# Four PSUM banks instead of two for the dense products behind the attention stage of a hybrid decoder layer

## The chip, the cores and the metric

The kernel runs on one core of one Trainium2 chip. The metric is device time in microseconds (us) of one execution; less is better. Engines are named as in the profile: PE (matrix products), DVE (VectorE), ACT (ScalarE), POOL (GpSimd), SP (SyncE, which here only issues DMAs).

## What is computed

One decoder layer over 1024 tokens of width 1024, in float32. A normalised input `h` goes through one wide projection; its columns feed an RWKV-7 time mixing, a causal depthwise convolution of width 31 with LayerNorm, and a cross-attention into 256 memory tokens. Each branch is projected back to 1024 columns, the three are merged by sigmoid gates, and an output projection with a residual and a final RMSNorm ends the layer. What matters here is the end:

```python
u = ((uf - um) * lax.rsqrt(uv + LN_EPS) * ln_g + ln_b)
u = jax.nn.silu(u) * jax.nn.silu(conv_gate)
y_conv = u @ w_proj_conv + b_proj_conv
...
y_mem = (att * jax.nn.silu(mem_gate)) @ w_proj_mem
gates = jax.nn.sigmoid(merge_logits).reshape(B, S, N_BRANCH, D_MODEL)
y = gates[:, :, 0] * y_rwkv + gates[:, :, 1] * y_conv + gates[:, :, 2] * y_mem
return x + y @ w_out, v_first
```

## The kernel before

Every dense product is one call of `g_dense` for one tile of 128 output columns. Operands are split into a high part and a low part (`hH`, `hL` for the input, `wh`, `wl` for the weight tile), and three matmuls per block of the inner dimension (high by high, low by high, high by low) keep float32 precision. A tile has two halves of 512 tokens (`e` = 0, 1). One half is a **group** here: 24 matmuls of 128x512 that add up in one PSUM bank `po`. The function `done` that is passed in then reads the bank (it evicts it, on ACT, DVE or both), and only after that may PE write the bank again.

PSUM has eight banks. `bank(tag, bufs)` (line 74) hands them out by tag: `d` 2, `g` 2, `ry` 2, `tr` 1, `sas` 1. All dense products use `d`, so a group's first matmul waits until the group two before it is evicted. Tag `g` serves the RWKV stage, the memory keys (line 870), the scores (line 938), the transposes of the probabilities (line 963) and the attention product (line 978); behind the attention nobody asks for it.

The weights come through `Stream`: a DMA brings `wf` (one buffer), ACT copies it to `wh` (line 123), DVE subtracts to `wl` (line 124). There are two buffers of `wh` and `wl`; the next tile's split is issued in the middle of a tile (`stream.ahead`).

From the last attention job on (`("att", 3)`) the program has five stages, and the numbers of groups below run over the first four:

- **cg**, groups 1 to 12: six tiles of the convolution gate. `done_cg` evicts with a tanh on ACT (line 927) and a DVE product (928), then writes to DRAM. Beside it run the last taps of the convolution (DVE, line 841) and `g_stats`: the channel mean (two products of PE into `ry`, line 995, that need `csum` from POOL, line 848) and the variance, column tile by column tile (`xs`: a load, DVE line 1006, ACT line 1008, POOL line 1013). The loads of `o_mem_d` are split into `oH`, `oL` (ACT line 270, DVE line 271).
- **pm**, groups 13 to 28: the memory projection. `done_pm` (line 1101) multiplies by the gate on DVE and writes `y1`. Beside it `g_ln` normalises 16 half tiles `xv`: loads, DVE lines 1047, 1051, 1056, 1058, ACT lines 1054, 1055, 123, POOL line 124.
- **pc**, groups 29 to 44: the convolution projection, on the output of `g_ln`. `done_pc` evicts on ACT (line 1138), then DVE. Beside it the loads of `o_rwkv_d` (one buffer `ost`) are split by ACT line 270 and DVE line 271, and half of the output weights (`woH`, `woL`).
- **pr**, groups 45 to 60: the RWKV projection, evicted by DVE (line 1157).
- **wo**: the output product, 16 groups of 24 matmuls through `mm3` (line 212), evicted by DVE (line 1189).

Within one engine the instructions run in the order in which they stand. That order is made when the program is built: the generators are interleaved by written costs, and the framework then orders the instructions engine by engine.

Of the kernel before, what the change touches and what calls it, by code (L numbers as in the profile page):

```python
# [62 lines left out]
def hybrid_kernel(ctx: ExitStack, tc: tile.TileContext, x: bass.AP, mem: bass.AP, wt: bass.AP,  # L63
# [10 lines left out]
    def bank(tag, bufs=1):  # L74
        return ps.tile([P, HS], F32, name=tag, tag=tag, bufs=bufs)
# [37 lines left out]
    def rsqrt(out_ap, in_ap, mul, add):  # L113
        pool.tensor_scalar(out=out_ap, in0=in_ap, scalar1=mul, scalar2=add, op0=ALU.mult, op1=ALU.add)
        p0 = in_ap.shape[0]
        n = in_ap.shape[1]
        base = 0 if p0 == P else P - p0
        pool.tensor_tensor(out=out_ap, in0=out_ap, in1=nhalf[base:P, 0:n], op=ALU.pow)
# [88 lines left out]
    def mm3(po, terms):  # L207
        n = 3 * len(terms)
        i = 0
        for (lh, ll, rh, rl) in terms:  # L210
            for l, r in ((lh, rh), (lh, rl), (ll, rh)):
                pe.matmul(po, lhsT=l, rhs=r, start=(i == 0), stop=(i == n - 1))  # L212
                i += 1
# [52 lines left out]
    def g_load_o(op, src, scale, oH, oL, dt):  # L266
        for k in range(KT):
            st = op.tile([P, S], F32, name="ost", tag="ost", bufs=1)
            nc.sync.dma_start(out=st, in_=src[k])
            act.activation(oH[:, k, :], st, AF.Copy, scale=scale)  # L270
            dve.scalar_tensor_tensor(out=oL[:, k, :], in0=st, scalar=scale, in1=oH[:, k, :].bitcast(F32),  # L271
                                     op0=ALU.mult, op1=ALU.subtract)
            yield dt

    def split_tiles(op):
        return op.tile([P, KT, S], F32R, name="oH"), op.tile([P, KT, S], F32R, name="oL")


    def g_dense(idx, done, rh=None, rl=None, pre=None):
        wh, wl = stream.get(idx)  # L280
        rh, rl = (hH, hL) if rh is None else (rh, rl)
        for e in range(2):
            if pre is not None:
                pre(e)
            po = bank("d", 2)
            sl = slice(e * HS, (e + 1) * HS)
            n = 0
            for k in range(KT):
                ks_ = slice(k * P, (k + 1) * P)
                for l, r in ((wh, rh), (wh, rl), (wl, rh)):  # L290
                    pe.matmul(po, lhsT=l[:, ks_], rhs=r[:, k, sl], start=(n == 0), stop=(n == 3 * KT - 1))  # L291
                    n += 1
                    if n % 4 == 0 and n < 3 * KT:
                        yield
            if e == 0:
                stream.ahead()
            done(e, po)
            yield
# [21 lines left out]

    late = {}
    lo_gen = g_dense(T_LO, lambda e, po: late["lo"](e, po))
    with tc.tile_pool(name="prep", bufs=1, reuse_waits="tile") as pl:
        for i, _ in enumerate(g_norm(x, S, "g_norm", pl, hH, hL)):
# [4 lines left out]
    with tc.tile_pool(name="rk", bufs=1, reuse_waits="tile") as rk:  # L329
# [103 lines left out]
        def tile_job(kind, j):  # L433
            if kind == "lo":
                late["lo"] = done_lo
                return lo_gen
            if kind == "k":
                return g_dense(T_K + j, done_shift(KS, j, T_K, "ks", 2))
            if kind == "r":
                return g_dense(T_R + j, done_shift(RS, j, T_R, "rs", 3))  # L440
            if kind == "v":
                return g_dense(T_V + j, done_shift(VS, j, T_V, "v", 2))
            if kind == "g":
                return g_dense(T_RG + j, done_sg(j))
            return g_dense(T_M0 + j, done_m(j))
# [347 lines left out]
    def later(name, gen):  # L793
        lanes.setdefault(name, [0.0, []])[1].append(gen)

    def run(gen):
        for dt in gen:
            background(dt or 0.85)
# [9 lines left out]
    def opened(stack, name, **kw):  # L808
        return stack.enter_context(tc.tile_pool(name=name, bufs=1, reuse_waits="tile", **kw))
# [255 lines left out]
    for n_, i_ in att_jobs:  # L1065
        run(g_dense(kinds[n_] + i_, done[n_](i_)) if n_ in done else other[n_](i_))
        if (n_, i_) == ("att", 3):
            at_stack.close()
            kv_stack.close()
            pm = AT["pm"] = opened(pm_stack, "pm")  # L1070
            mean = pm.tile([P, S], F32, name="mean")
            rstd = pm.tile([P, S], F32, name="rstd")
            AT["ones"] = pm.tile([P, P], F32, name="ones")
            dve.memset(AT["ones"], 1.0)
            omH, omL = split_tiles(pm)
            later("conv", g_stats(mean, rstd))
            later("load", g_load_o(pm, o_mem_d, 0.5, omH, omL, 6.0))
# [38 lines left out]
    def g_wo(pl, fh, hi, lo, dt):  # L1116
        fs = slice(fh * HS, (fh + 1) * HS)
        for k in range(KT):
            st = w0.tile([P, HS], F32, name="wst", tag="wst", bufs=2)
            nc.sync.dma_start(out=st, in_=wt[T_WO + k][:, fs])  # L1120
            split_sb(st, hi[:, k, :], lo[:, k, :])
            yield dt

    def wo_tiles(pl):
        return pl.tile([P, KT, HS], F32R, name="woH"), pl.tile([P, KT, HS], F32R, name="woL")
# [42 lines left out]
    with tc.tile_pool(name="wo1", bufs=1, reuse_waits="tile") as w1:  # L1168
        wo.append(wo_tiles(w1))
        gf = w1.tile([P, D], F32, name="gf")  # L1170
        nc.scalar.dma_start(out=gf, in_=gfin.broadcast_to([P, D]))
        xr = []
        for t in range(KT):
            xt = w1.tile([P, D], F32, name=f"xr{t}")
            nc.scalar.dma_start(out=xt, in_=x[t * P:(t + 1) * P, :])
            xr.append(xt)
        ss = w1.tile([P, KT, 2], F32, name="fss")
        e0 = w1.tile([P, KT], F32, name="fe")
        rs = w1.tile([P, KT], F32, name="frs")
        g1 = g_wo(w1, 1, *wo[1], 0.0)  # L1180
        for fh in range(2):
            fs = slice(fh * HS, (fh + 1) * HS)
            oh, ol = wo[fh]
            for t in range(KT):
                tl = slice(t * P, (t + 1) * P)
                po = bank("d", 2)
                mm3(po, [(yH[:, k, tl], yL[:, k, tl], oh[:, k, :], ol[:, k, :]) for k in range(KT)])
                next(g1, None)
                dve.tensor_tensor(out=xr[t][:, fs], in0=xr[t][:, fs], in1=po, op=ALU.add)
                sq = w1.tile([P, HS], F32, name="sq", tag="sq", bufs=2)  # L1190
                act.activation(sq, xr[t][:, fs], AF.Square, accum_out=ss[:, t, fh:fh + 1])
                if fh == 0:
                    pool.tensor_scalar(out=e0[:, t:t + 1], in0=ss[:, t, 0:1], scalar1=1.0 / D, scalar2=RMS_EPS,
                                       op0=ALU.mult, op1=ALU.add)
                if fh == 1:
                    rsqrt(rs[:, t:t + 1], ss[:, t, 1:2], 1.0 / D, e0[:, t:t + 1])
                    for h_ in range(2):
                        hs_ = slice(h_ * HS, (h_ + 1) * HS)
                        dve.scalar_tensor_tensor(out=xr[t][:, hs_], in0=xr[t][:, hs_], scalar=rs[:, t:t + 1],
                                                 in1=gf[:, hs_], op0=ALU.mult, op1=ALU.mult)  # L1200
                        (nc.sync, nc.scalar)[h_].dma_start(out=out[tl, hs_], in_=xr[t][:, hs_])
# [45 lines left out]
```

## Time and profile before

| | before |
|---|---|
| median of 3 runs | 1961.04 us (1960.19 to 1962.81) |
| the profiled execution, its own time | 1960.84 us |
| its span in the trace | 1959.0 us |
| PE busy | 1848.2 us, 94% |
| DVE busy | 1411.1 us, 72% |
| ACT busy | 693.2 us, 35% |
| POOL busy | 226.5 us, 12% |
| mean clock granted to PE | 0.991 |

PE is the busiest engine by far, and its matmuls are pipelined: the busy time counts each from its own start to its modelled end. What a stage loses on PE is therefore read from the idle time before a matmul and from the start of one group to the start of the next. The span lies 1.84 us under the execution's own time.

### The profile page before, as it was taken

To read this page: it belongs to the slowest core of one execution; us is meant where nothing else is said; L and a number is where in the kernel's file an instruction comes from. 1 tells how busy PE (TensorE), PEld (TensorE's weight loads), DVE (VectorE), ACT (ScalarE), POOL (GpSimd) and SP (SyncE) were. 2 spreads that over 40 slices of the span, in tenths; PEclk is the share of its full clock that TensorE was granted. 3 is DMA by queue.
4 is the path that set the end of the run, shared out by engine and by line. 5 is a ranking of instruction groups with operands and counts; after the bars stand their busy time and mean duration, and the time that the engine had idled before them with its cause. 6 is when DMAs were issued, how large, how long until landed. Compare 5 with 4: busy or idle time off the path is not lost. (4 is left out here: it accounts for less than half of the span.)

```text
span 1959.0 us, 30018 instructions
## 1 busy us (share of the span) xinstructions
PE 1848.2 (94%) x11412; PEld 1472.8 (75%) x11412; DVE 1411.1 (72%) x3028; ACT 693.2 (35%) x1303; POOL 226.5 (12%) x311
## 2 busy tenths in 40 slices
PE   6999998989899899989999999999999999999998
PEld 5777766767676676667788888888888787778887
DVE  6667787777778777787636998898999748644423
ACT  6334343443344344334334313232313435432121
POOL 2201111111111111111000000000000213100001
PEclk9999999999999999999999999999999999999999
DMA  4232212122121212212224411212123646775332
GB/s 147 58 97 63 71 36 68 54 61 68 48 86 36 66 56 58 71 42 79 71 78 140 132 46 42 75 54 76 54 76 108 233 163 221 256 252 164 129 129 86
DMA packets 127936, 188.61 MB, mean 96 GB/s; under 512 B 64432, under 2 KB 66608, under 8 KB 127792
## 3 DMA queue, kind: packets, MB, share of 16 engines
q1 hardware_dynamic: 122704, 178.11, 29.0%
q10 hardware_dynamic: 4768, 8.07, 1.1%
q8 instruction: 89, 1.46, 0.3%
q0 software_dynamic: 320, 0.52, 0.1%
q14 instruction: 55, 0.45, 0.1%
HBM read 139.92 MB, written 46.20 MB: 95 GB/s over the span
## 5 line engine op out<-in xcount | busy, mean ns | idle before, releaser
L291 PE MATMUL d<-hH,wh 128*128 128x512 f32 x1552 | 626.0, 403 | 6.8 <-DVE cg L928 4.4
L291 PE MATMUL d<-hH,wl 128*128 128x512 f32 x1552 | 621.8, 401 | 0.0
L291 PE MATMUL d<-hL,wh 128*128 128x512 f32 x1552 | 619.1, 399 | 0.0
L291 PEld LDWEIGHTS d<-hH,wh 128*128 128x128 f32 x1552 | 294.1, 189 | 63.6 <-DVE cg L928 5.7
L291 PEld LDWEIGHTS d<-hH,wl 128*128 128x128 f32 x1552 | 294.1, 190 | 59.4 <-issue 0.2
L291 PEld LDWEIGHTS d<-hL,wh 128*128 128x128 f32 x1552 | 294.1, 189 | 56.2 <-issue 0.2
L841 DVE SCALAR_TENSOR_TENSOR ac<-up,wdw,ac 128x1024 f32<-128x1024 f32 x240 | 308.2, 1284 | 11.8 <-ACT ac L838 6.0
L123 ACT CAST wh<-wf 128x1024 fp32r<-128x1024 f32 x137 | 143.6, 1049 | 324.1 <-PE d L291 304.3
L124 DVE TENSOR_TENSOR wl<-wf,wh 128x1024 fp32r<-128x1024 f32 x137 | 176.8, 1291 | 95.7 <-ACT wh L123 95.4
L291 PE MATMUL d<-oH,wh 128*128 128x512 f32 x384 | 152.5, 397 | 11.4 <-DVE mg L1101 7.4
L291 PE MATMUL d<-oH,wl 128*128 128x512 f32 x384 | 151.4, 394 | 0.0
L291 PE MATMUL d<-oL,wh 128*128 128x512 f32 x384 | 151.4, 394 | 0.0
L583 DVE TENSOR_TENSOR W<-W,tm 128x60 f32<-128x60 f32 (+24 forms) x496 | 112.4, 227 | 10.0
L580 DVE TENSOR_TENSOR tm<-W,U 128x60 f32<-128x60 f32 (+24 forms) x496 | 107.7, 217 | 11.1
L706 ACT ACTIVATE sp<-s,pc 128x128 f32<-128x128 f32 x120 | 48.3, 402 | 174.8 <-DVE s L713 137.6
L291 PEld LDWEIGHTS d<-oH,wh 128*128 128x128 f32 x384 | 72.9, 190 | 30.4 <-ACT y L1138 5.1
L710 PEld LDWEIGHTS sas<-sav,tk 128*128 128x128 f32 x240 | 38.4, 188 | 67.5 <-DVE sav L703 49.2
L710 PE MATMUL sas<-sav,tk 128*128 128x128 f32 x240 | 54.1, 307 | 34.1 <-DVE sav L703 32.4
L291 PEld LDWEIGHTS d<-oH,wl 128*128 128x128 f32 x384 | 72.8, 190 | 16.1
L291 PEld LDWEIGHTS d<-oL,wh 128*128 128x128 f32 x384 | 72.8, 189 | 15.4
L713 DVE SCALAR_TENSOR_TENSOR s<-sas,pc,sp 64x64 f32<-64x64 f32 x240 | 67.6, 282 | 21.5 <-PE sas L710 16.1
L703 DVE TENSOR_TENSOR sav<-ry,Y 64x128 f32<-64x128 f32 x128 | 36.8, 288 | 43.4 <-ACT Y L668 26.5
(277 smaller groups left out, 2608.7 us busy)
## 6 DMA issues: line engine op xcount, KB each, us to landing
wf<-in_wt_dram SPq DMA_DIRECT2D x137, 512.0 KB
g_d<-gt SPq DMA_DIRECT2D x48, 256.0 KB
U<-ud SPq DMA_DIRECT2D x64, 128.0 KB
nxt<-in_x_dram SPq DMA_DIRECT2D x8, 512.0 KB
o_rwkv_d<-o SPq DMA_DIRECT2D x16, 256.0 KB
cv_d<-ac SPq DMA_DIRECT2D x8, 512.0 KB
o_mem_d<-om SPq DMA_DIRECT2D x16, 256.0 KB
xs<-cv_d SPq DMA_DIRECT2D x8, 512.0 KB
```

Of the source, the lines that this page charges most:

```text
L123: act.copy(hi, src)
L124: (eng or dve).tensor_tensor(out=lo, in0=src, in1=hi.bitcast(F32), op=ALU.subtract)
L291: pe.matmul(po, lhsT=l[:, ks_], rhs=r[:, k, sl], start=(n == 0), stop=(n == 3 * KT - 1))
L580: dve.tensor_tensor(out=tv, in0=W[:, 0:m, i:i + 1].broadcast_to([NG * 32, m, n]), in1=U[:, i:i + 1, i + 1:32].broadcast_to([NG * 32, m, n] ...
L583: dve.tensor_tensor(out=wv_, in0=wv_, in1=tv, op=ALU.add)
L703: dve.tensor_tensor(out=sav[own, cc, :], in0=ry[own, cs], in1=Y[own, c // 2, :], op=ALU.add)
L706: act.activation(sp, S0, AF.Copy, scale=pc[:, c:c + 1])
L710: pe.matmul(sn[:, 0:P], lhsT=tk[:, cc, :], rhs=sav[:, cc, :], start=True, stop=True)
L713: dve.scalar_tensor_tensor(out=S1[vsl, vsl], in0=sn[vsl, vsl], scalar=pc[vsl, c:c + 1], in1=sp[vsl, vsl], op0=ALU.mult, op1=ALU.add)
L841: dve.scalar_tensor_tensor(out=ac, in0=up[:, tap:tap + S], scalar=wdw[:, tap * 8 + j:tap * 8 + j + 1], in1=ac, op0=ALU.mult, op1=ALU.add)
```

## The change

A counter `banks` gives each dense group a tag in turn. Up to the last attention job the list of tags is `("d",)`, so nothing changes there. From then on it is `("d", "g")`: the groups alternate between the two banks of `d` and the two of `g`, and a group's first matmul waits for the eviction of the group four before it. `g_dense` and the output product both use it.

```diff
+    banks = {"n": 0, "tags": ("d",)}
+
+    def dense_bank():
+        banks["n"] += 1
+        return bank(banks["tags"][banks["n"] % len(banks["tags"])], 2)
+
     def g_dense(idx, done, rh=None, rl=None, pre=None):
...
-            po = bank("d", 2)
+            po = dense_bank()
...
         if (n_, i_) == ("att", 3):
             at_stack.close()
             kv_stack.close()
+            banks["tags"] = ("d", "g")
...
-                po = bank("d", 2)
+                po = dense_bank()
                 mm3(po, [(yH[:, k, tl], yL[:, k, tl], oh[:, k, :], ol[:, k, :]) for k in range(KT)])
```

The framework's order of instructions differs from before in one stretch only, the cg stage: on PE, DVE, ACT and SP. POOL's order is the same everywhere, and from the pm stage on so is that of the other engines, but for the name of the bank. Two places follow. In the changed kernel line numbers between 285 and 1069 are 7 higher, and 8 higher behind that.

PE, in group 5: the two products for the channel mean (`ry<-csum,ones`) between the group's matmuls. Before:

```order
L291 MATMUL d<-hH,wh 128x512
L291 MATMUL d<-hL,wh 128x512
L995 MATMUL ry<-csum,ones 128x512 x2
L291 MATMUL d<-hH,wl 128x512
L291 MATMUL d<-hH,wh 128x512
L291 MATMUL d<-hL,wh 128x512
```

Now:

```order
L298 MATMUL g<-hL,wh 128x512
L298 MATMUL g<-hH,wl 128x512
L298 MATMUL g<-hH,wh 128x512
L298 MATMUL g<-hL,wh 128x512
L1002 MATMUL ry<-csum,ones 128x512 x2
L298 MATMUL g<-hH,wl 128x512
```

The pair stood behind the eighth matmul of its group and now stands behind the eleventh.

DVE, in the cg stage, from the low part of the weights of its fifth tile (groups 9 and 10) to that of its sixth (`wl`; `xs` is the variance, `cg` an eviction, `oL` a split of `o_mem_d`). Before:

```order
L124 TENSOR_TENSOR wl<-wf,wh 128x1024
L1006 TENSOR_TENSOR xs<-xs,mean 128x1024
L928 SCALAR_TENSOR_TENSOR cg<-cg,d 128x512
L1006 TENSOR_TENSOR xs<-xs,mean 128x1024
L271 SCALAR_TENSOR_TENSOR oL<-ost,oH 128x1024
L124 TENSOR_TENSOR wl<-wf,wh 128x1024
L928 SCALAR_TENSOR_TENSOR cg<-cg,d 128x512
```

Now:

```order
L124 TENSOR_TENSOR wl<-wf,wh 128x1024
L1013 TENSOR_TENSOR xs<-xs,mean 128x1024
L271 SCALAR_TENSOR_TENSOR oL<-ost,oH 128x1024
L935 SCALAR_TENSOR_TENSOR cg<-cg,g 128x512
L1013 TENSOR_TENSOR xs<-xs,mean 128x1024
L271 SCALAR_TENSOR_TENSOR oL<-ost,oH 128x1024
L935 SCALAR_TENSOR_TENSOR cg<-cg,d 128x512
L1013 TENSOR_TENSOR xs<-xs,mean 128x1024
L124 TENSOR_TENSOR wl<-wf,wh 128x1024
L1013 TENSOR_TENSOR xs<-xs,mean 128x1024
```

Counted from the first `wl`, one `xs`, one `cg` and one `oL` more stand ahead of the second than before. The first `wl` itself has one `oL` less ahead of it, so the sixth tile's weights have moved behind one more `xs`, the sixth, and one more eviction.

## Rows read from the trace of the kernel before

**Rows 1.** Waits of PE, 1505 to 1960 us: us in total, times, longest.
```profile
PE d L291 <- DVE mg L1101: 7.4, 5, 2.8
PE d L291 <- DVE cg L928: 4.4, 3, 2.7
PE d L291 <- ACT y L1138: 4.0, 2, 2.6
```
**Rows 2.** Timeline of PE, cg stage: start, us; in brackets idle before and releaser.
```profile
1523.78 0.50 PE L291 MATMUL d<-hH,wh 128*128 128x512 f32 x1 [0.91 <-DVE cg L928]
1531.65 1.98 PE L995 MATMUL ry<-csum,ones 128*128 128x512 f32 x4 [0.30 <-POOL csum L848]
1561.74 0.50 PE L291 MATMUL d<-hH,wh 128*128 128x512 f32 x1 [2.69 <-DVE cg L928]
1575.34 0.50 PE L291 MATMUL d<-hH,wh 128*128 128x512 f32 x1 [0.78 <-DVE cg L928]
1580.91 0.40 PE L291 MATMUL d<-oH,wh 128*128 128x512 f32 x1
```
**Rows 3.** Timeline of PE, pm stage: first matmuls of groups 22 to 27.
```profile
1634.97 0.40 PE L291 MATMUL d<-oH,wh 128*128 128x512 f32 x1
1641.22 0.47 PE L291 MATMUL d<-oH,wh 128*128 128x512 f32 x1 [0.49 <-DVE mg L1101]
1648.35 0.50 PE L291 MATMUL d<-oH,wh 128*128 128x512 f32 x1 [1.30 <-DVE mg L1101]
1655.44 0.47 PE L291 MATMUL d<-oH,wh 128*128 128x512 f32 x1 [1.22 <-DVE mg L1101]
1662.82 0.50 PE L291 MATMUL d<-oH,wh 128*128 128x512 f32 x1 [1.56 <-DVE mg L1101]
1671.51 0.48 PE L291 MATMUL d<-oH,wh 128*128 128x512 f32 x1 [2.83 <-DVE mg L1101]
```
**Rows 4.** The same, pc stage: first matmuls of groups 30, 36, 38, 39 and 40.
```profile
1689.77 0.39 PE L291 MATMUL d<-oH,wh 128*128 128x512 f32 x1
1723.96 0.50 PE L291 MATMUL d<-oH,wh 128*128 128x512 f32 x1 [1.39 <-ACT y L1138]
1737.90 0.80 PE L291 MATMUL d<-oH,wh 128*128 128x512 f32 x1 [2.60 <-ACT y L1138]
1744.81 0.39 PE L291 MATMUL d<-oH,wh 128*128 128x512 f32 x1
1750.25 0.39 PE L291 MATMUL d<-oH,wh 128*128 128x512 f32 x1
```
**Rows 5.** Windows: busy us of each engine in each stretch, PEclk, DMA share, GB/s.
```profile
1560.00:1570.00 10.00, 8.26 (x29) 6.64 (x30) 6.95 (x6) 4.64 (x6) 3.49 (x2) 0.83 0.82 254
1670.00:1680.00 10.00, 8.49 (x30) 6.79 (x31) 9.44 (x12) 5.24 (x7) 3.25 (x3) 0.83 0.64 222
1736.00:1746.00 10.00, 8.10 (x30) 6.59 (x31) 5.13 (x8) 4.45 (x6) 0.00 (x0) 0.83 0.80 250
1780.00:1790.00 10.00, 10.00 (x45) 8.13 (x44) 2.75 (x5) 0.97 (x2) 0.00 (x0) 1.00 0.57 184
```
**Rows 6.** Timeline of POOL and DVE, cg stage.
```profile
1529.19 2.40 POOL L848 TENSOR_TENSOR csum<-csum,ac 128x1024 f32<-128x1024 f32 x1 [60.52 <-DVE ac L841]
1561.60 1.21 DVE L1006 TENSOR_TENSOR xs<-xs,mean 128x1024 f32<-128x1024 f32 x1
1573.47 1.21 DVE L124 TENSOR_TENSOR wl<-wf,wh 128x1024 fp32r<-128x1024 f32 x1
```
**Rows 7.** Timeline of DVE and ACT, pm and pc: weights, and what stands beside them.
```profile
1663.38 1.23 DVE L124 TENSOR_TENSOR wl<-wf,wh 128x1024 fp32r<-128x1024 f32 x1 [0.62 <-ACT wh L123]
1669.12 1.65 DVE L1047 TENSOR_TENSOR xv<-xv,mean 128x512 f32<-128x512 f32 x1 [1.00 <-DMA xv<-cv_d]
1677.97 1.73 DVE L124 TENSOR_TENSOR wl<-wf,wh 128x1024 fp32r<-128x1024 f32 x1
1725.11 1.22 DVE L124 TENSOR_TENSOR wl<-wf,wh 128x1024 fp32r<-128x1024 f32 x1
1734.78 1.23 DVE L124 TENSOR_TENSOR wl<-wf,wh 128x1024 fp32r<-128x1024 f32 x1 [3.25 <-ACT wh L123]
1736.22 1.06 ACT L270 ACTIVATE oH<-ost 128x1024 fp32r<-128x1024 f32 x1 [1.47 <-DMA ost<-o_rwkv_d]
```

## The prediction

> **What bounds the kernel now.** I read the waits of PE first, from the end of the attention on. All of PE's idle time at the dense products there is laid to three evictions: 7.4 us behind `mg`, 4.4 behind `cg`, 4.0 behind `y`, ten waits and 15.8 us together [rows 1]. The timeline then shows where: three in cg [rows 2], five in pm [rows 3], two in pc [rows 4]. Each stands before the first matmul of a group, so it is the bank of the group two before that was not yet read. In pr and wo there is none: PE runs without idle time at 1780 to 1790 [rows 5].
>
> The windows show a second loss. Around the three longest waits (2.69, 2.83, 2.60 us) the granted clock is 0.83 over 10 us, against 1.00 in a stretch without waits [rows 5]: the clock fell from 2.4 to 1.2 GHz for a while, and each time 0.17 x 10 = 1.7 us of work at full rate is lost, 5.1 together. The wait of 1.56 us [rows 3] has no such fall behind it (the windows name just three).
>
> A third, small loss is the restart. Group 24 starts 7.13 us after group 23, of which 1.30 is the wait ahead of it [rows 3]; from group 22 to 23 it is 6.25 with a wait of 0.49. An undisturbed group takes 5.6 in this stage, so about 0.22 are lost beside the wait; ten waits make 2.2. In pc an undisturbed group takes 1750.25 - 1744.81 = 5.44 [rows 4], which is 0.227 for each of 24 matmuls.
>
> So the whole loss that hangs on the banks is 15.8 + 5.1 + 2.2 = 23.1 us. What the change gives is this less what PE meets next.
>
> **The change, part by part.** It adds and removes no instruction that computes or moves data; no durations change. It lets PE be four groups ahead of the evictions instead of two. The banks of `g` are free: the attention product is their last user. In pr and wo I cost it at nothing, since PE does not wait there. A group's eviction takes 0.6 to 0.7 us on one engine; the lateness comes from the queues in front of it, and they stay. So I walk along PE from group to group and ask at each tile whether the bank or the weights (`wl`, which the third matmul of a tile reads, 0.47 after its first) come last.
>
> *cg.* The three waits go: 0.91 + 2.69 + 0.78 = 4.4, with one fall of the clock 1.7 and three restarts 0.7, 6.8 in all. Part of the first comes back at once. The products for the channel mean wait for `csum`, which POOL ends at 1529.19 + 2.40 = 1531.6 [rows 6] whatever PE does. PE gets there 0.91 + 0.22 earlier, but three matmuls (0.68) now stand ahead that stood behind, so its wait grows from 0.30 to 0.75: 0.45 back. Next are the weights of group 11. Their `wl` stands behind the sixth `xs` now, which ran at 1561.60 for 1.21 [rows 6]; with 1.2 for itself `wl` ends by 1564.0. Group 11 would start at 1563.7 (group 13 at 1580.91 - 6.35 [rows 2], less two groups of 5.44) and needs it at 1564.2: no wait, but no room either. The weights of group 13 ended at 1573.47 + 1.21 = 1574.7 [rows 6], and are needed at 1580.91 - 6.35 + 0.47 = 1575.0 [rows 2]: again just in time. Of 6.35 I take **6.0**; the bounds are 3 (each of these two late by some 1.6, an `xs` with its load) and 6.35.
>
> *pm and pc, in the times of before.* What DVE and ACT do here is started by PE once: the variance goes through two small products between groups 14 and 17, where PE does not wait, so the whole chain of `g_ln` comes earlier by the 6.0 of cg and no more. From there DVE sets its own pace: at 1670 to 1680 it is busy 9.44 of 10 us [rows 5], and its gaps are waits for loads of `xv` [rows 7]. ACT in pc is held by the loads of `o_rwkv_d`, one behind the other through one buffer, and the evictions and weights stand behind them in its queue [rows 7]. So I leave every time of DVE and ACT as it is and move PE alone:
>
> - Group 23 starts at 1634.97 + 5.6 = 1640.6, groups 24 to 26 follow without a wait (the evictions that they need now are two groups older; the worst of before was 2.83 late, two groups are 11.2). Group 27 starts at 1663.0.
> - It opens a tile, and its `wl` ends at 1663.38 + 1.23 = 1664.6 [rows 7]. Needed at 1663.4: 1.2 lost and 0.2 for the restart. Group 29 starts at 1663.0 + 11.2 + 1.4 = 1675.6.
> - Its `wl` ends at 1677.97 + 1.73 = 1679.7 [rows 7], needed at 1676.0: 3.7 + 0.2 lost. Group 30 starts at 1675.6 + 5.4 + 3.9 = 1684.9; before it was 1689.77 [rows 4]. Here 4.9 are gained.
> - Groups 31 to 36 take 5.44 each; the waits ahead of groups 36 and 38 (1.39 and 2.60) were for banks that are no longer needed then. Group 37 starts at 1723.0. Its `wl` ends at 1725.11 + 1.22 = 1726.3 [rows 7], needed at 1723.5: 2.9 + 0.2 lost.
> - Group 39 starts at 1736.9; its `wl` is there at 1734.78 + 1.23 = 1736.0 [rows 7]. Group 40 starts at 1742.4, and the eviction that it needs is the one that let group 38 go at 1737.9 before. Before, group 40 started at 1750.25 [rows 4]: **7.8** gained, with no wait behind it.
>
> So of ten waits for banks three come back as waits for weights, at groups 27, 29 and 37. The last two are long enough for the clock to fall (2.60 was, 1.56 was not). After group 29 that would be made up by the wait at group 37; after group 37 it would cost 1.7, which leaves 6.1. I take 7.8, since the wait at 37 comes in two pieces, for `wh` and for `wl`.
>
> Sum: 6.0 + 7.8 = **13.8 us** off the profiled execution's 1960.84, whose span is 1959.0; it lies 0.2 under the median of the runs, 1961.04. Forecast for the median: **1947.2 us**. The bounds of the terms, 3 + 6.1 and 6.35 + 7.8, give 1947 to 1952.
>
> **The rivals.**
>
> *A, every wait goes and nothing takes its place.* All but 0.45 of 23.1: 1938.4 us. For it: no wait for weights is among PE's rows now [rows 1]. Against it: those weights were on time only because PE was late, and at group 29 the row misses by 3.7. The Trainium skill ("Perfetto Trace Analysis", Optimizing Tensor Performance, Matmuls) says that independent groups should rotate through banks so that the evacuation of one overlaps the next; by that alone this would be the outcome. The rows with `wl` speak against it. Chance 0.10.
>
> *B, the wait is renamed.* DVE and ACT are the pace, and PE, let off the banks, waits for weights at nearly every tile from group 25 on; only the first cg waits are gained, some 3 us: 1958. For it: the weights of groups 27, 29 and 37 are already late in my walk. Against it: those of group 39 and of all later tiles are not, and in pc the bank that PE needs is two groups older. The Trainium skill ("TensorE: Matmul & The Clock Gate", HAM oscillation — how this bites in real kernels) tells of a kernel in which PSUM double-buffering gave no further gain; by that case it would be 1961. Rows 1 disagree, for here PE does wait for banks. Chance 0.07.
>
> *C, slower: the new order on DVE in cg.* The weights of group 11 now stand behind the sixth `xs`, those of group 13 behind the eighth as before. An `xs` hangs on a load, ACT and POOL: sixth to eighth took 10.7 us (1561.60 to the `wl` directly behind the eighth at 1573.47, less 1.2) [rows 6], 5.4 each. If this chain slips, PE stands, and its clock falls too. Three steps late make 3 x 5.4 + 3 x 1.7 = 21.3, against 13.8 won: 1968.5. It decides from two steps on (14.2). Against it: the chain's loads depend on POOL, whose order is unchanged. Chance 0.03.
>
> **How the numbers follow.** My forecast has 0.80. About 0.2% (3.9 us) is what a measurement of this kernel can tell from no change. B lies within that, C above; so faster 0.90, same 0.07, slower 0.03. For the range I take 1941.5 to 1953: below, half way to A; above, the bound of 1952 and a little.
>
> **What would show it.** Right: PE's waits for `cg`, `mg` and `y` are gone or under 2 us together; new waits of PE stand at groups 27, 29 and 37 with ACT `wh` or DVE `wl` as releaser, some 8 us in all; the wait at the channel mean is near 0.75; stage pm starts 6 us earlier and group 40 nearly 14; pr and wo take as long as before. Wrong: waits for `mg` or `y` still there (then the evictions lag by more than four groups); waits for weights in cg (rival C); no waits at groups 27 and 29 (rival A, with DVE earlier than I leave it); or the granted clock below 1.00 in more than three places.

## The result, and the profile after

| | before | the change | ratio (95%) |
|---|---|---|---|
| median, first comparison | 1962.29 us (1960.19 to 1962.91, 6 runs) | 1949.73 us (1945.27 to 1951.05, 6 runs) | 0.9933 (0.9920 to 0.9946) |
| median, repeated | 1961.70 us (1957.44 to 1966.86, 17 runs) | 1951.38 us (1948.09 to 1953.43, 6 runs) | 0.9946 (0.9930 to 0.9961) |
| the profiled execution of the first | 1960.84 us, span 1959.0 | 1949.77 us, span 1947.8 | |
| mean clock granted to PE | 0.991 | 0.993 | |

The changed kernel is faster by 12.6 us in the first comparison and by 10.3 in the second. The forecast was 1947.2 us, with a range of 1941.5 to 1953.

The span is 11.2 us shorter. Where these went is read from the first matmuls of groups 1, 13, 30 and 40, the places at which the prediction counts the gain. The stretches between them are called cg, pm and pc here; the second holds all of pm and the first group of pc:

| us | cg (1 to 13) | pm (13 to 30) | pc (30 to 40) | group 40 to the end |
|---|---|---|---|---|
| before | 74.56 | 108.86 | 60.48 | 208.75 |
| the change | 68.79 | 105.00 | 58.58 | 208.55 |
| gained | 5.8 | 3.9 | 1.9 | 0.2 |

Together that is 11.7; group 1 itself starts 0.5 later than before, ahead of anything that the change touches. Two falls of the clock fewer than before (one in place of three, some 1.7 us each) are a part of the gain.

The waits of PE in the changed kernel from 1490 to 1960 us (us in total, times, longest), which answer to [rows 1]:

```profile
PE g L298 <- ACT wh L123: 5.3, 3, 2.2
PE g L298 <- DVE wl L124: 2.1, 3, 1.2
PE ry L1002 <- POOL csum L855: 1.0, 1, 1.0
```

Not one wait for `cg`, `mg` or `y` is left; 7.4 us of waits for weights stand there instead. The timeline of PE shows where. These lines are the beginnings of groups 1 and 13, the channel mean, then the first and third matmuls of groups 27, 29 and 37 and the first of groups 30 and 40; they answer to [rows 2 to 4]:

```profile
1506.88 0.40 PE L298 MATMUL g<-hH,wh 128*128 128x512 f32 x1
1532.32 1.98 PE L1002 MATMUL ry<-csum,ones 128*128 128x512 f32 x4 [0.99 <-POOL csum L855]
1575.67 0.40 PE L298 MATMUL g<-oH,wh 128*128 128x512 f32 x1
...
1659.13 0.50 PE L298 MATMUL g<-oH,wh 128*128 128x512 f32 x1 [1.24 <-ACT wh L123]
1660.39 0.50 PE L298 MATMUL g<-oH,wl 128*128 128x512 f32 x1 [0.53 <-DVE wl L124]
1673.55 0.50 PE L298 MATMUL g<-oH,wh 128*128 128x512 f32 x1 [2.16 <-ACT wh L123]
1675.51 0.51 PE L298 MATMUL g<-oH,wl 128*128 128x512 f32 x1 [1.23 <-DVE wl L124]
1680.67 0.39 PE L298 MATMUL d<-oH,wh 128*128 128x512 f32 x1
1720.83 0.68 PE L298 MATMUL g<-oH,wh 128*128 128x512 f32 x1 [1.92 <-ACT wh L123]
1722.31 0.79 PE L298 MATMUL g<-oH,wl 128*128 128x512 f32 x1 [0.38 <-DVE wl L124]
1739.25 0.39 PE L298 MATMUL d<-oH,wh 128*128 128x512 f32 x1
```

Each of the three tiles waits twice: for the rounded weights `wh`, which ACT makes, and 1.3 to 2.0 us later for the remainder `wl`, which DVE makes from `wh`. The timelines of POOL, DVE and ACT say why these are late (they answer to [rows 7]). At group 29 it begins with an operation of `g_ln` on DVE, which takes 1.67 us at 1670.23, while POOL works. ACT's cast of `oH` waits 1.95 us for it, and the cast of `wh` stands behind that one and ends at 1672.45 + 1.04 = 1673.49. Then `wl` ends at 1673.74 + 1.71 = 1675.45, again beside an operation of POOL. At group 37 the cast of `wh` stands on ACT behind the cast of `ost`, which waits 1.22 us for its load.

```profile
1670.06 1.29 POOL L124 TENSOR_TENSOR oL<-xv,oH 128x512 fp32r<-128x512 f32 x1 [4.10 <-ACT oH L123]
1672.62 1.74 POOL L124 TENSOR_TENSOR oL<-xv,oH 128x512 fp32r<-128x512 f32 x1 [1.28 <-ACT oH L123]
...
1670.23 1.67 DVE L1065 TENSOR_TENSOR xv<-xv,lsg 128x512 f32<-128x512 f32 x1
...
1673.74 1.71 DVE L124 TENSOR_TENSOR wl<-wf,wh 128x1024 fp32r<-128x1024 f32 x1
...
1671.93 0.62 ACT L123 CAST oH<-xv 128x512 fp32r<-128x512 f32 x1 [1.95 <-DVE xv L1065]
1672.45 1.04 ACT L123 CAST wh<-wf 128x1024 fp32r<-128x1024 f32 x1
...
1718.21 1.06 ACT L270 ACTIVATE oH<-ost 128x1024 fp32r<-128x1024 f32 x1 [1.22 <-DMA ost<-o_rwkv_d]
...
1719.74 1.03 ACT L123 CAST wh<-wf 128x1024 fp32r<-128x1024 f32 x1
```

The windows around the three tiles, columns as in [rows 5]:

```profile
1657.00:1667.00 10.00, 8.23 (x34) 6.05 (x33) 7.97 (x10) 5.03 (x7) 3.10 (x2) 1.00 0.63 224
1672.00:1682.00 10.00, 7.23 (x30) 5.67 (x31) 5.31 (x7) 4.86 (x7) 3.03 (x2) 1.00 0.77 238
1718.00:1728.00 10.00, 7.70 (x28) 5.47 (x27) 6.69 (x8) 4.82 (x6) 0.00 (x0) 0.83 0.88 288
```

The granted clock stays at 1.00 around groups 27 and 29 and falls at group 37 (0.83, so 1.7 us of work at full rate). The matmuls at 1720.83 and 1722.31 show it singly: 0.68 and 0.79 us, where the others take 0.50 or 0.51. The fall comes behind the first piece of that wait: from 1721 to 1722 us the granted clock is 0.50, and the second piece ends only at 1722.31.

### The profile page after: what moved, and what is told of

Same layout as the page of the kernel before. It is cut to its first block, busy times and chain, and to the rows that moved or that the text cites. A ratio compares the mean times of both kernels' runs of the same rounds, so it can differ in the third digit from the quotient of the medians.

```text
span 1947.8 us, 30024 instructions
## 1 busy us (share of the span) xinstructions
PE 1844.5 (95%) x11412; PEld 1472.2 (76%) x11412; DVE 1410.6 (72%) x3028; ACT 691.9 (36%) x1303; POOL 227.7 (12%) x311
## 4 chain that ended last, share of the span: by engine, by line
PE 63%; DVE 23%; DMA 4%; issue 4%; ACT 3%; POOL 3%; SPq 0%; DVEq 0%; POOLq 0%; ACTq 0%
PE d L298 41%; PE g L298 5%; PE g L212 4%; DVE W L590 3%; DVE tm L587 3%; PE d L212 2%; DVE s L720 2%; PE g L552 2%; DVE wl L124 2%; DVE sav L710 1%; PE ry L894 1%; POOL vr L118 1%; DVE Y L761 1%; DVE Y L738 1%; PE sas L717 1%
## 5 line engine op out<-in xcount | busy, mean ns | idle before, releaser
L298 PE MATMUL d<-hH,wh 128*128 128x512 f32 x1504 | 607.2, 404 | 2.4 <-ACT lc L383 2.0
L298 PE MATMUL d<-hH,wl 128*128 128x512 f32 x1504 | 603.0, 401 | 0.0
L298 PE MATMUL d<-hL,wh 128*128 128x512 f32 x1504 | 600.1, 399 | 0.0
L298 PEld LDWEIGHTS d<-hH,wl 128*128 128x128 f32 x1504 | 285.0, 189 | 56.9
L587 DVE TENSOR_TENSOR tm<-W,U 128x60 f32<-128x60 f32 (+24 forms) x496 | 107.7, 217 | 11.1
L298 PE MATMUL g<-oH,wh 128*128 128x512 f32 x192 | 76.3, 398 | 5.3 <-ACT wh L123 5.3
L298 PE MATMUL g<-oH,wl 128*128 128x512 f32 x192 | 76.2, 397 | 2.1 <-DVE wl L124 2.1
L298 PE MATMUL g<-oL,wh 128*128 128x512 f32 x192 | 75.8, 395 | 0.0
L298 PE MATMUL d<-oL,wh 128*128 128x512 f32 x192 | 75.2, 392 | 0.0
L298 PE MATMUL d<-oH,wl 128*128 128x512 f32 x192 | 75.2, 392 | 0.0
L298 PE MATMUL d<-oH,wh 128*128 128x512 f32 x192 | 75.2, 392 | 0.0
```

The lines of the kernel that those rows point to most:

```text
L587: dve.tensor_tensor(out=tv, in0=W[:, 0:m, i:i + 1].broadcast_to([NG * 32, m, n]), in1=U[:, i:i + 1, i + 1:32].broadcast_to([NG * 32, m, n] ...
```

## The experiments

Every expectation was written before its run. The questions were: does each half of the switch give its own term; is it the banks, or only the order in which the scheduler puts the instructions of the changed kernel; and who makes the evictions and the weights late. The edits are edits of the changed kernel unless the text says otherwise. Four banks in cg alone, the first run of four banks from pm on, three banks, and the change with the split on DVE ran on one chip (before 1961.23 us there). The others ran on a second chip: the last of all in a later session (before 1962.0), the rest together (before 1961.70). Stages are read from one traced execution each.

**Four banks in cg alone.**

```diff
-    drain("load")
+    drain("load"); banks["tags"] = ("d",)
```

> Four banks in the cg stage only, two again from pm on. Theory (each stage gives back its own bank waits): the gain of cg stays, some 6 us, and the waits for mg and y in pm and pc are back (some 11 us with two falls of the clock), so about 1956 us. Rival (the gain comes from the new order of DVE, ACT and SP in cg, not from the banks behind it): nearly all of the 12.6 us stays, 1950. In the trace: waits of PE for mg and y as in the kernel before, none for cg.

Measured: 1956.25 us (10 runs), ratio 0.9971 (0.9958 to 0.9984), so 5.0 us are gained, as the theory said. cg takes 68.22 us, as in the change; pm and pc take 109.18 and 57.34. The waits of PE from 1490 to 1960 us:

```profile
PE d L298 <- DVE mg L1109: 7.8, 5, 2.8
PE d L298 <- ACT y L1146: 2.0, 2, 1.8
PE ry L1002 <- POOL csum L855: 0.9, 1, 0.9
```

The waits for `cg` are gone, and the five for `mg` stand as before (7.4 in [rows 1], 7.8 here). For `cg` and `mg` the banks act where they are given, and only there. In pc two banks lost less in this execution than before (60.48 us there): the waits for `y` are 2.0 us, where [rows 1] has 4.0, and the clock doesn't fall there. It is the shortest of the ten (1951.35 us), so the pc stage of a single trace can be 3 us off for another reason than the banks.

**Four banks from pm on alone**, and the same again with more runs:

```diff
-            banks["tags"] = ("d", "g")
...
-    drain("load")
+    drain("load"); banks["tags"] = ("d", "g")
```

> Two banks in cg, in the old order, and four from pm on. Theory: the three cg waits stay, the waits for mg and y go, and weights come late at groups 27, 29 and 37 as in the change: 6 to 8 us won, about 1955 us. Rival (order in cg makes the gain): nothing won, 1962.

> Four banks from pm on, timed again. The trace of the first run has pm and pc 6.75 us shorter than before, its times only 2.9 us less (0.4 to 6). Theory (the trace is right, the times scatter with what happens ahead of cg): 5 to 7 us under the kernel before. Rival (what pm and pc win is given back outside of them): 2 to 4 us again, and a longer stretch elsewhere in the trace.

Measured: 1958.35 us, ratio 0.9984 (0.9971 to 0.9998), 2.9 us gained; then 1956.93 us (12 runs), ratio 0.9974 (0.9962 to 0.9985), 4.8 us gained. The first is less than expected; the second lies a little under its expectation, into which its interval (2.9 to 7.5 us) reaches. The stages of the two traces say the same twice: pm and pc together take 162.59 and 163.12 us, where before has 169.34, so 6.7 and 6.2 less. In both traces group 1 starts later than in the trace of before, by 2.8 and 3.2 us (1509.16 and 1509.53 against 1506.35), ahead of what the edit touches, so that 3.9 and 3.3 us are left in the spans. The traces of the other kernels have group 1 between 1504.95 and 1509.65; what moves it was not settled. The waits in the second:

```profile
PE d L298 <- DVE cg L935: 4.3, 3, 2.7
PE g L298 <- ACT wh L123: 3.8, 2, 2.2
PE g L298 <- DVE wl L124: 2.0, 3, 0.8
...
```

Now the three waits of cg are back (4.4 in [rows 1]), and the weights are late in pm and pc although cg was not shortened. So the late weights of pm and pc don't need PE's earlier start from cg: they were late before, hidden by the waits for banks. The two halves sum to 5.0 + 2.9 = 7.9 us on the first chip, or 5.0 + 4.8 = 9.8 with the second measurement, beside 10.3 for the whole on the second chip. The rival by which a new order alone gives the gain falls for pm and pc: in the traces of this kernel DVE, ACT and POOL run their operations in the order of before throughout, and PE does from cg on, yet the waits for `mg` and `y` are gone. In cg the new order and the banks come together, and nothing tells them apart.

**Three banks**: the third is the bank of the transposes, `tr`, with one buffer.

```diff
-        return bank(banks["tags"][banks["n"] % len(banks["tags"])], 2)
+        tag = banks["tags"][banks["n"] % len(banks["tags"])]; return bank(tag, 1 if tag == "tr" else 2)
...
-            banks["tags"] = ("d", "g")
+            banks["tags"] = ("d", "tr", "d")
```

> Three banks in rotation from the attention on (the two of d and the one of tr). Theory: the evictions that PE waited for were at most 2.83 us late, a third bank gives 5.4 us, so almost everything goes with it; by the walk of the prediction groups 28 and 39 would wait some 1 us for a bank: 1950 to 1951 us, not to be told from the change. Rival (PE uses the full four groups of lead): waits for mg and y come back in half, 1954 or more.

Measured: 1951.60 us, ratio 0.9949 (0.9933 to 0.9965), 9.6 us gained. The waits for banks come to 1.5 us, where two banks have 15.8 and four none. They stand at groups 13 and 29, not at 28 and 39 as expected:

```profile
PE d L298 <- ACT wh L123: 4.1, 2, 3.0
PE ry L1002 <- POOL csum L855: 2.4, 1, 2.4
PE tr L298 <- DVE mg L1109: 1.0, 1, 1.0
PE d L298 <- DVE wl L124: 0.9, 2, 0.5
PE tr L298 <- DVE wl L124: 0.8, 1, 0.8
PE d L298 <- DVE cg L935: 0.5, 1, 0.5
```

One bank more gives nearly all of it: four banks came to 1949.73 and 1951.38 us in the two measurements of the change, and what the fourth is worth these runs can't tell from nothing.

**The change, with the split of `g_ln` on DVE instead of POOL.** In `g_ln` the remainder `oL` of each normed tile was POOL's: 16 operations of 128x512.

```diff
-                split_sb(x_, cH[:, j, sl], cL[:, j, sl], eng=pool)
+                split_sb(x_, cH[:, j, sl], cL[:, j, sl], eng=dve)
```

> The change, and the low part of the normalised conv output (16 products of 128x512 in g_ln) on DVE in place of POOL. Theory (DVE is late with the weights because its own operations stand still while POOL runs, 1.65 us in place of 0.69, and the chain through POOL is long): without POOL in that chain the waits for weights at groups 27 and 29 shrink to under 1 us each although DVE gets 16 x 0.6 = 9.6 us more to do, and the pc stage begins some 5 us earlier: 1941 to 1946 us. Rival (DVE is plainly full, 94% busy at 1670 to 1680): 9.6 us more on it make the weights later still, 1954 us or more.

Measured: 1941.21 us (1938.59 to 1942.54, 4 runs), ratio 0.9893 (0.9865 to 0.9920), 20.0 us gained, as the theory said. pm takes 98.71 us, where the change has 105.00, and no weight is late at groups 27 and 29. PE runs without a gap through the middle of pm; the windows of before, of the change and of this kernel, one after the other, columns as above:

```profile
1605.00:1680.00 75.00, 67.61 (x288) 53.05 (x287) 61.88 (x83) 40.10 (x55) 22.50 (x15) 0.98 0.62 210
```
```profile
1605.00:1680.00 75.00, 69.84 (x297) 55.20 (x296) 59.39 (x75) 37.21 (x52) 24.10 (x16) 1.00 0.66 213
```
```profile
1605.00:1680.00 75.00, 75.00 (x326) 60.65 (x325) 63.54 (x98) 41.65 (x56) 0.00 (x0) 1.00 0.73 238
```

DVE does 98 operations in the time in which it did 83 before, and is busy only 1.7 us longer (63.54 against 61.88): its operations have become shorter. By line and form from 1600 to 1690 us (busy, mean ns of one | idle ahead and its releaser), first before, then this kernel:

```profile
L1047 DVE TENSOR_TENSOR xv<-xv,mean 128x512 f32<-128x512 f32 x13 | 14.1, 1083 | 6.5 <-DMA xv<-cv_d 6.5
L1058 DVE TENSOR_TENSOR xv<-xv,lsg 128x512 f32<-128x512 f32 x16 | 12.9, 809 | 0.3
...
L1101 DVE SCALAR_TENSOR_TENSOR mg<-mg,d 128x512 f32<-128x512 f32 x14 | 9.6, 682 | 11.7 <-PE d L291 7.6 <-DMA mg<-g_d 4.1
L124 DVE TENSOR_TENSOR wl<-wf,wh 128x1024 fp32r<-128x1024 f32 x7 | 9.5, 1364 | 1.2 <-ACT wh L123 1.2
...
L124 POOL TENSOR_TENSOR oL<-xv,oH 128x512 fp32r<-128x512 f32 x16 | 23.8, 1489 | 62.2 <-ACT oH L123 62.2
```
```profile
L1065 DVE TENSOR_TENSOR xv<-xv,lsg 128x512 f32<-128x512 f32 x16 | 10.9, 688 | 0.7 <-DMA lsg<-sc_d 0.4
...
L124 DVE TENSOR_TENSOR oL<-xv,oH 128x512 fp32r<-128x512 f32 x16 | 10.8, 685 | 0.1
L124 DVE TENSOR_TENSOR wl<-wf,wh 128x1024 fp32r<-128x1024 f32 x8 | 9.8, 1221 | 0.3 <-ACT wh L123 0.3
L1054 DVE TENSOR_TENSOR xv<-xv,mean 128x512 f32<-128x512 f32 x13 | 9.0, 689 | 5.6 <-DMA xv<-cv_d 5.6
```

The mean of the subtraction falls from 1083 to 689 ns, that of `lsg` from 809 to 688, that of `wl` from 1364 to 1221. Single operations of 128x512 that took up to 1.78 us in the trace of before (1.65 in [rows 7]) now take 0.69. The timelines of the trace of before tell when an operation is stretched. Twelve operations of `g_ln` and `wl` with both inputs in SBUF began while an `oL` of POOL was under way: all twelve were stretched, by 0.48 to 1.10 us, 9.1 together. Ten more overlapped one but had begun ahead of it, and 43 ran without POOL: none of these was. The Trainium skill ("SBUF — State Buffer", Who interferes with whom) says that DVE and GpSimd share one pair of ports as an exclusive lock, so that a DVE instruction with both inputs in SBUF stands still while a GpSimd instruction reads SBUF. These rows agree: the three operations named have both inputs in SBUF, and the excess goes when POOL's operations do. The evictions `mg`, which read one of their inputs from PSUM, are the control: five of them began under an `oL` of POOL, and all 14 took 0.67 to 0.69 us. The edit also takes POOL out of the chain that frees the buffers of `xv`; DVE's waits for those loads only fall from 6.5 to 5.6 us, so this is the smaller part.

**The kernel before, with that edit alone** (two banks, its line 1059):

> Two banks everywhere, and only the 16 low parts of g_ln on DVE in place of POOL. Theory (PE's bank waits in pm are DVE's lateness, and that comes from standing still behind POOL): the five waits for mg, 7.4 us, nearly go even with two banks, one fall of the clock with them; cg and pc keep theirs: 1951 to 1956 us. Rival (only the banks can take the waits away, DVE stays as late): 1958 to 1963.

Measured: 1953.01 us (1948.05 to 1954.34), ratio 0.9952 (0.9935 to 0.9968), 8.7 us gained, as the theory said. The waits:

```profile
PE d L291 <- DVE cg L928: 3.5, 2, 2.6
PE d L291 <- ACT y L1138: 2.9, 3, 2.0
...
```

The five waits for `mg` are gone with two banks. pm takes 98.71 us, as with four banks and the same edit. So in pm two banks suffice for an evicting engine that is on time, and the extra banks cover, in part, for DVE being held up by POOL. In cg and pc the banks keep their worth: 73.37 and 60.71 us with two, 69.16 and 56.23 with four, in one trace each. That it is the ports that hold DVE up was not tried by a run of its own; what speaks for it is that `mg` isn't stretched.

**More off POOL**: besides the split, the sums `vs` in `g_stats` and the last addition to `csum` go to DVE.

```diff
-            pool.tensor_tensor(out=csum, in0=csum, in1=ac, op=ALU.add)
+            (dve if j == 7 else pool).tensor_tensor(out=csum, in0=csum, in1=ac, op=ALU.add)
...
-                    pool.tensor_tensor(out=vs, in0=vs, in1=x_, op=ALU.add)
+                    dve.tensor_tensor(out=vs, in0=vs, in1=x_, op=ALU.add)
...
-                split_sb(x_, cH[:, j, sl], cL[:, j, sl], eng=pool)
+                split_sb(x_, cH[:, j, sl], cL[:, j, sl], eng=dve)
```

> The change, and beside the low parts of g_ln also the sums of the variance (7 of 128x1024) and the last sum of the channel mean on DVE in place of POOL (2.4 us there, about 1.2 on DVE). Theory: csum is ready some 1.2 us earlier, so the wait at the channel mean (0.9) goes, and the weights of group 11 (0.6 late with the low parts alone) are on time: 1 to 4 us under the change with the low parts alone, which was 1941.2. Rival (DVE is full in cg, 7 sums more on it make evictions and weights late): 1942 or more.

Measured: 1939.97 us (1937.46 to 1941.23, 5 runs), ratio 0.9886 (0.9870 to 0.9903). This is the shortest time of the study, 11.4 us under the change on the same chip. Of all of PE's waits from 1490 to 1950 us one is left, 0.5 us for `wl`; cg takes 67.11 us, 2.05 less than with the split alone, where `wl` of group 11 was 0.63 us late and `csum` 0.89. In time it lies 1.2 us below that kernel, which ran on another chip, and their runs overlap: whether these two additions are worth anything by themselves stays open.

**The change again**, on the second chip; its times stand in the first table. It gained 10.3 us, a little less than the 11 to 13 expected.

> The change itself once more, beside the parts on one chip. Theory: 11 to 13 us under the kernel before, weights late at groups 27, 29 and 37, no wait for an eviction.

Its stages: cg 68.27, pm 107.20, pc 55.76 us. cg agrees with the first trace; pm and pc differ singly, but their sum (162.96) is within 0.6 us of the first (163.58). In this execution the clock fell once from cg to group 40 too, but from 1678 us on, behind the waits of group 29 (2.18 and 1.23 us), not at group 37, where the only wait is 0.75 us, for `wl`.

**`o_rwkv`'s cast in pc on POOL instead of ACT**, and the high part of the output weights likewise (their low part stays on DVE), to bring `wh` forward on ACT:

```diff
-            act.activation(oH[:, k, :], st, AF.Copy, scale=scale)
+            pool.tensor_scalar(out=oH[:, k, :], in0=st, scalar1=scale, scalar2=None, op0=ALU.mult) if dt == 7.0 else act.activation(oH[:, k, :], st, AF.Copy, scale=scale)
...
-            split_sb(st, hi[:, k, :], lo[:, k, :])
+            pool.tensor_copy(hi[:, k, :], st) if dt else act.copy(hi[:, k, :], st)
+            dve.tensor_tensor(out=lo[:, k, :], in0=st, in1=hi[:, k, :].bitcast(F32), op=ALU.subtract)
```

> The change, with the high parts of the o_rwkv and output-weight loads of pc (8 of 128x1024, 8 of 128x512) on POOL in place of ACT; POOL is idle there. Theory (the weights of group 37 are late because wh stands behind casts on ACT that wait for loads): the wait for wh at group 37 (1.92, and a fall of the clock) goes; the waits at 27 and 29 stay; pc 2 to 4 us shorter, about 1947 to 1950 us beside 1951. Rival (the lateness comes from the loads themselves and moves to DVE, whose low parts of the same loads stand ahead of wl, or to POOL, which is slower): a wait for wl of 2 us or more in pc instead, 1950 to 1954.

Measured: 1962.17 us (1957.55 to 1966.11, 10 runs), ratio 0.9999 (0.9987 to 1.0010): the whole gain of the change is lost. Neither time that was written held. The rival's mechanism is what happened, and it cost more than the rival said. The third matmuls of groups 35, 37 and 39 in the timeline of PE, and DVE and POOL ahead of the first of them:

```profile
1715.10 0.79 PE L298 MATMUL g<-oH,wl 128*128 128x512 f32 x1 [2.93 <-DVE wl L124]
1730.88 0.50 PE L298 MATMUL g<-oH,wl 128*128 128x512 f32 x1 [3.02 <-DVE wl L124]
1746.92 0.80 PE L298 MATMUL g<-oH,wl 128*128 128x512 f32 x1 [3.22 <-DVE wl L124]
...
1709.88 2.77 POOL L270 TENSOR_SCALAR oH<-ost 128x1024 fp32r<-128x1024 f32 x1 [4.31 <-DMA ost<-o_rwkv_d]
1712.68 1.22 DVE L271 SCALAR_TENSOR_TENSOR oL<-ost,oH 128x1024 fp32r<-128x1024 f32 x1 [4.04 <-POOL oH L270]
1713.83 1.22 DVE L124 TENSOR_TENSOR wl<-wf,wh 128x1024 fp32r<-128x1024 f32 x1
```

The cast takes 2.77 us on POOL, 1.06 on ACT; the one buffer `ost` is held that much longer, DVE stands 4.04 us for it with `wl` next in its queue, and PE stands for `wl`. pc takes 70.34 us instead of 58.58. The wait for `wh` at group 37 is gone, as meant: it was moved from one queue to a slower chain. The three waits make 9.2 us, and the clock falls in or behind each of them: in windows of 10 us from 1711, 1728 and 1743 it is 0.83, 0.83 and 0.66, together some 6.8 us of work at full rate. A second buffer for `ost` was not tried.

## Why the prediction was right

- **The banks.** Of "the whole loss that hangs on the banks", 23.1 us, the 15.8 us of waits went to nothing. Rival B (waits renamed at nearly every tile) falls, as three tiles wait and no others; rival C falls, as no weight is late in cg in the two traces of the change. How little room there is shows with the split on DVE, where `wl` of group 11 is 0.63 us late.
- **cg, 6.0.** Measured 5.8 in the first trace, 6.3 in the repeat (74.56 less 68.27), and alone 5.0 us in time. The wait at the channel mean grew to 0.99 us, 0.75 was said.
- **The waits that come back, 1.2 + 3.7 + 2.9 = 7.8.** Measured 1.77 + 3.39 + 2.30 = 7.46, at groups 27, 29 and 37 as said, first for `wh`, then for `wl`. Rival A, by which all waits go, falls here. Evictions now overlap the next groups, but the same queues bring the weights.
- **pm and pc, 7.8: mis-sized.** 5.8 in the first trace, 6.4 in the repeat. Two things make the 2.0 us that are missing from the first, about 1.0 each. At group 30, 4.9 were to be gained and 3.9 were. "I leave every time of DVE and ACT as it is" let DVE's chain come earlier by all that cg gains, 5.8 here; but `wl` of group 29 ended at 1675.45, against 1679.70 before, which is only 4.8 earlier counted from group 1. Up to the `lsg` at 1609.61 DVE does run 5.8 earlier. The subtraction at 1618.93 is 5.0 earlier, since it waits 1.28 us for its load of `xv`, where the same subtraction had no wait before; later loads take the other 0.2. Why that load came late was not settled. The subtraction before, then now:

```profile
1623.42 0.69 DVE L1047 TENSOR_TENSOR xv<-xv,mean 128x512 f32<-128x512 f32 x1
...
1618.93 0.69 DVE L1054 TENSOR_TENSOR xv<-xv,mean 128x512 f32<-128x512 f32 x1 [1.28 <-DMA xv<-cv_d]
```

The other 1.0 is lost in pc (1.9 gained of 2.9). The prediction took no fall of the clock at group 37, "since the wait at 37 comes in two pieces". In this execution the first piece, 1.92 us, was enough: the clock fell behind it, which costs 1.7, while the wait itself was 0.6 shorter than said (2.30 for 2.9). That is the alternative of 6.1 that the prediction named and set aside. In the repeat the wait at group 37 was short and the fall came behind group 29 (2.18 and 1.23 us): again one fall between cg and group 40, not none.
- **pr and wo, nothing.** 208.75 and 208.55 us.
- **The sum.** 13.8 was said for the profiled execution; between the two traced executions it is 11.1 (1960.84 to 1949.77), between the medians 12.6 and 10.3. Of the 2.7 that the traces lack, pm and pc make 2.0, cg 0.2, and the later start of group 1 0.5. The forecast's range held both medians; its middle, 1947.2, was too low by 2.5 and 4.2 us.

What the prediction did not see is the cause behind the lateness that it took as given. It read DVE as busy 9.44 of 10 us in pm [rows 5] and took that for work. Some 2 us of it (an estimate: two operations of 1.65 us that take 0.69 without POOL, and a `wl` of 1.73 that takes 1.22) were DVE held up beside POOL, inside instructions that the profile counts as busy; taking POOL out of that chain is worth 8.7 us with two banks, and with four banks it brings the time from some 1951 to 1941 us.

## What to carry to other kernels

When PE waits for PSUM banks, walk on from the bank to the next thing that the same late queue delivers: here the weights' rounding stands behind the evictions on DVE and ACT, and 7.4 of 15.8 us came back as waits for it. Then ask why that queue is late: compare the mean of an operation in the stage with its shortest instance, and if an operation of 0.69 us averages 1.08, look for a neighbour before adding buffers. Banks and a punctual evictor are not alternatives everywhere: in pm the second made the first needless, in cg and pc the banks kept some 4 us in each, by one trace of either kernel.

## What the runs showed of the hardware

- DVE operations with two inputs in SBUF that began while POOL ran a subtraction on SBUF were stretched, 12 of 12 (from 0.69 to as much as 1.78 us for 128x512); those that had begun ahead of it were not, 0 of 10, nor those with one input in PSUM, 0 of 5. Giving DVE POOL's 16 operations (1.49 us each there, 0.685 on DVE) makes the stage shorter by 10.2 us (108.86 to 98.71).
- The length of PE's waits alone does not tell when its granted clock falls. It fell in or behind single waits of 2.60, 2.69 and 2.83 us (before), of 2.04 (before, with the split on DVE) and of 1.92 (the change, group 37), and behind 1.10 and 0.53 us close together (three banks, group 27). It did not fall behind 1.56 (before), 1.80 (four banks in cg alone), or 1.24 and 0.53 (the change, group 27). Behind 2.16 and 1.23 it stayed at 1.00 in the first trace of the change, and behind 2.18 and 1.23 at the same place it fell in the repeat.
- A cast of 128x1024 with a scale takes 2.77 us on POOL and 1.06 on ACT.
